# Second half of an RWKV-7 layer's projections in another order: gates first, rates among the keys

## The chip, the cores and the metric

The kernel runs on one core of one Trainium2 chip. The metric is the device time of one execution in microseconds. A core has five engines that run side by side, each with its own queue of instructions in a fixed order: PE multiplies matrices (PEld loads its stationary operands), DVE, ACT and POOL work elementwise, and SP here issues the transfers between memory and the chip. An instruction waits on semaphores for what it needs, and all instructions behind it in the same queue wait with it.

## The reference, cut to what matters

The program computes two layers over 1024 tokens of width 1024 in float32: an RWKV-7 time mixing layer and a diagonal state-space layer, each followed by a squared-ReLU MLP and a layer norm. The change is in the projections of the first one:

```python
xx = jnp.pad(x, ((0, 0), (1, 0), (0, 0)))[:, :-1] - x
xr = x + xx * mu[0]                      # and xw, xk, xv, xa, xg with mu[1..5]
r = xr @ wr
w_pre = (w0 + jnp.tanh(xw @ w1) @ w2)
decay = jnp.exp(-jnp.exp(-jax.nn.softplus(-w_pre) - 0.5))
k = xk @ wk
v = xv @ wv
a = jax.nn.sigmoid(a0 + (xa @ a1) @ a2)
g = jax.nn.sigmoid(xg @ g1) @ g2
```

Then a recurrence over the tokens uses `r`, `decay`, `k`, `v` and `a` per head, its output is normalised, multiplied by `g` and by `wo`. In the kernel the "rates" are the two small products with `w2` and `a2` (64 rows each) and the sigmoids after them, the "gates" are `g`, the "keys" are `k`, and R is `r`.

## The kernel before, in words

All activations lie transposed, features on the partitions. The 1024 tokens are worked in two halves of 512 (`H` is 0 or 1), and the 1024 features in eight tiles of 128 (`KT`). Every dense product is made in float32 precision from three products of split operands: `split` (L145 to L147) makes a high part with a copy on ACT (L146) and a low part with a subtraction on DVE (L147), and `mm3` (L177) issues high by high, high by low and low by high. All of them are recorded on L175. `wload` (L158) brings weights in pieces of 256 KB into `wraw` (two buffers) and splits them into `whi` and `wlo` (three buffers each).

`rwkv_proj(H)` (L229) makes the projections of one half. It splits the input `xs` into eight pairs of operands (`xo`), and from these makes the inner products of the rates and gates (`shifted`, L310, and `scaled`, L295): the source of the rates is `hd`, split into `hx` (L335); those of the gates are `gx` and `h2` (L355 and L336). Then come the outer products. `rates(n)` (L369) makes six matmuls on halves of the array, into two PSUM banks, and for each bank a tanh on ACT (L380), a half-sigmoid on POOL (L325) and a store (L365). `gate(n)` (L384) makes four matmuls, one copy on ACT (L397) and a store. `square(wn, out, xm, n)` (L400) makes the 24 matmuls of one tile of keys or R from the operands `xm`, a copy (L404) and a store. `mixes(j)` (L263) makes these operands: a product on ACT (L266), a multiply-add on DVE (L268) or two steps on POOL (L271, L272), and a split. The results go to memory (`s_sg`, `s_a`, `s_g`, `s_k`, `s_r`, `s_v`) and are loaded again by the units that use them.

Buffers are rings that hand out a slot when its last reader has finished. PSUM has three banks `d` for the dense products (`psd`, L214). Results on their way out, and the POOL part of `mixes`, share three buffers `ev`. For the second half the operand pairs `xo`, `hx`, `gx`, `h2` and later `xm` share one ring of eight high and eight low tiles (`oAh`, `oAl`, `optile`, L204). For the first half `hx` and the others stand in spare buffers of the recurrence (`spare`, L251).

The recurrence is worked in eight units (`core`, L757), four for each half of the tokens. A unit loads its rates, keys and R and prepares them (`elem`, L474), makes its score matrices (`amat`, L551), inverts triangular blocks, mostly on DVE (`invert`, L585), and steps through a chain of small matmuls (`chain`, L645). A unit of the second half needs the second half's projections. The kernel is ordered when it is built: a planner simulates a timeline, and gives each engine the instruction that is ready by that simulation and has the lowest number. Numbers grow in program order, and `rank` (L86) sets where they start. The units have numbers up to about 80000; the projections of the second half start at 100000 and stand in the program before unit 3 (L771 to L773), so they are filler beside the chains of units 2 and 3. The MLP of the first half of the tokens starts at 200000 and fills in later; the first half's `wo` has 99000.

Of the kernel before, what the change touches and what calls it, by code (L numbers as in the profile page):

```python
# [19 lines left out]
KT = 8  # L20
# [50 lines left out]
def trunk(ctx, tc, A):  # L71
# [13 lines left out]
    @contextmanager  # L85
    def rank(base):  # L86

        keep = tc.cur_priority
        tc.cur_priority = base
        yield  # L90
        tc.cur_priority = keep
# [53 lines left out]
    def split(src, hi, lo, e=None):  # L145
        S.copy(hi, src)  # L146
        (e or V).tensor_sub(lo, src, hi.bitcast(F32))  # L147
# [10 lines left out]
    def wload(src, kt, n):  # L158
        step = 512 // n
        out = []  # L160
        for k0 in range(0, kt, step):
            raw = wp.tile([128, step, n], F32, tag="wraw", name="wraw", bufs=2)
            SP.dma_start(raw, src[:, k0 : k0 + step])
            hi = wp.tile([128, step, n], F32R, tag="whi", name="whi")
            lo = wp.tile([128, step, n], F32R, tag="wlo", name="wlo")
            nw[0] += 1
            split(raw, hi, lo, G if nw[0] % WLG[0] in WLG[1] and WLG[2] <= nw[0] < WLG[3] else V)
            out += [(hi[:, k], lo[:, k]) for k in range(step)]
        return out
# [4 lines left out]
    def mmb(p, w, x, **kw):  # L174
        bulk.append((PE.matmul(p, w, x, **kw).ins, x.shape[-1]))  # L175
# [23 lines left out]
    def dense(p, w, xs):  # L199
        n = len(xs)  # L200
        for k in range(n):
            mm3(p, w[k][0], w[k][1], xs[k][0], xs[k][1], k == 0, k == n - 1)

    def optile(H, hl):  # L204
        if H == 1:
            return sp.tile([128, HT], F32R, tag="oB" + hl, name="oB" + hl, bufs=8)
        return ap.tile([128, HT], F32R, tag="oA" + hl, name="oA" + hl, bufs=8)
# [6 lines left out]
    def psd():  # L214
        return pd.tile([128, HT], F32, tag="d", name="d")
# [13 lines left out]
    def rwkv_proj(H):  # L229
# [21 lines left out]
        def spare(tag, n, bufs, pool=kp):  # L251
            t = pool.tile([128, n, HT], F32R, tag=tag, name="oS", bufs=bufs)
            return [t[:, k] for k in range(n)]

        def spare0():
            t = spare("vsa", 2, 2) + spare("vsa", 2, 2)
            for _ in range(4):
                t += spare("kbt", 1, KTB)
            t += [stash[:, k, l] for k in (1, 2, 3) for l in range(2)]
            t += spare("o", 1, OB) + spare("o", 1, OB)  # L260
            return [(t[2 * k], t[2 * k + 1]) for k in range(KT)]

        def mixes(j, dst=None):  # L263
            for k in range(KT):
                m = tp.tile([128, HT], F32, tag="m", name="m")
                S.mul(m, xs[k][:, 1:], mum[:, j, k : k + 1])  # L266
                if k % 4 in VM[H]:
                    V.scalar_tensor_tensor(m, xs[k][:, 0:HT], vec(f"mu{j}", k), m, op0=ALU.mult, op1=ALU.add)  # L268
                else:
                    m2 = tp.tile([128, HT], F32, tag="ev", name="m2", bufs=3)  # L270
                    G.tensor_scalar(m2, xs[k][:, 0:HT], vec(f"mu{j}", k), None, op0=ALU.mult)  # L271
                    G.tensor_add(m, m, m2)  # L272
                if dst:
                    split(m, *dst[k])
                    yield dst[k]
                else:
                    yield operand(m)
# [46 lines left out]
        def half_sigmoid(t):  # L324
            G.tensor_scalar(t, t, 0.5, 0.5, op0=ALU.mult, op1=ALU.add)  # L325
# [3 lines left out]
        if H == 0:  # L329
            stash = ap.tile([128, 2 * KB2, 2, HT], F32R, tag="q", name="stash", bufs=1)  # L330
            hx = stash[:, 0, 0], stash[:, 0, 1]
            gx, h2 = spare("gt", 1, GTB) + spare("lg", 1, LGB), spare("la", 1, 2, tp)[0]
        else:
            hx, gx, h2 = [(optile(0, "h"), optile(0, "l")) for _ in range(2)] + [optile(0, "h")]
        split(hd, *hx)  # L335
        def gate_c():  # L336

# [26 lines left out]
        def store_out(out, n, e):  # L364
            (ST if out in STO else SP).dma_start(scr[out][n * 128 : (n + 1) * 128, t0 : t0 + HT], e)  # L365
# [3 lines left out]
        def rates(n):  # L369

            if n % 4 == 0:
                w2[0] = wload(A["wa2"][:, n // 4], 4, 128)
            pp = [psd(), psd()]
            for wi, xi in ((0, 0), (0, 1), (1, 0)):
                for j in range(2):
                    js = slice(64 * j, 64 * j + 64)
                    mmb(pp[j], w2[0][n % 4][wi][js], hx[xi][js], start=wi == 0 and xi == 0, stop=wi == 1)
            for j, out in ((0, "sg"), (1, "a")):
                e = tp.tile([128, HT], F32, tag="ev", name="ev", bufs=3)
                S.activation(e, pp[j], AF.Tanh, bias=pvh[:, j, n : n + 1], scale=0.5)  # L380
                half_sigmoid(e)
                store_out(out, n, e)

        def gate(n):  # L384
            if n % 4 == 0:
                wg[0] = wload(A["g2a"][:, n // 4], 4, 128)
                rawb = wp.tile([128, 512], F32, tag="wraw", name="w2raw", bufs=2)
                SP.dma_start(rawb, A["g2b"][:, n * 128 : n * 128 + 512])
                wg[1] = wp.tile([128, 512], F32R, tag="whi", name="w2st")
                S.copy(wg[1], rawb)  # L390
                V.tensor_sub(wg[1][64:128], rawb[64:128], wg[1][64:128].bitcast(F32))
            q = n % 4
            p = psd()
            mm3(p, wg[0][q][0], wg[0][q][1], gx[0], gx[1], True, False)
            mmb(p, wg[1][:, q * 128 : (q + 1) * 128], h2, start=False, stop=True)
            e = tp.tile([128, HT], F32, tag="ev", name="ev", bufs=3)
            S.copy(e, p)  # L397
            store_out("g", n, e)

        def square(wn, out, xm, n):  # L400
            p = psd()
            dense(p, wload(A[wn][n], KT, 128), xm)
            e = tp.tile([128, HT], F32, tag="ev", name="ev", bufs=3)
            S.copy(e, p)  # L404
            store_out(out, n, e)

        if H == 0:

            km = xm
            with rank(MIX0R):  # L410
                rm = list(mixes(0, spare0()))
            for n in range(4):
                rates(n)
                square("wk", "k", km, n)
            for n in range(4):
                square("wr", "r", rm, n)
            yield
            for n in range(4, KT):
                rates(n)
                square("wk", "k", km, n)  # L420
            for n in range(4, KT):
                square("wr", "r", rm, n)
            if not GV:
                for n in range(KT):
                    gate(n)
        else:
            for n in range(KT):
                rates(n)
            for n in range(KT):
                gate(n)  # L430
            xm = list(mixes(2))
            for n in range(KT):
                square("wk", "k", xm, n)
            xm = list(mixes(0))
            for n in range(KT):
                square("wr", "r", xm, n)
# [320 lines left out]
    def core():  # L757

        pg = rwkv_proj(0)
        next(pg)  # L760
        bulk.clear()
# [8 lines left out]
        for m in range(8):  # L770
            if m == PB:  # L771
                with rank(100000):
                    run(rwkv_proj(1))  # L773
# [591 lines left out]
```

## Time and profile before

| | |
|---|---|
| median of 3 runs | 2767.67 us (2766.5 to 2772.65) |
| profiled execution | 2764.91 us |
| its span, first to last instruction | 2763.2 us |
| mean granted clock of PE | 0.958 |
| PE busy | 2604.9 us, 94% |
| DVE busy | 1884.5 us, 68% |
| ACT busy | 1109.5 us, 40% |
| POOL busy | 719.6 us, 26% |
| stores of the second half's rates | 349 to 392 us |
| of its gates, keys, R | 391 to 411, 455 to 497, 522 to 584 us |

A profile is one execution taken by the hardware profiler. Times are in microseconds from the span's start. In a row of the timeline stand start, duration, engine, line, operation, the tile written and those read, the shape and how many; in square brackets the idle time of the engine before it and what ended it. In a group's row stand busy time, the mean of one in nanoseconds, and the idle time before them with what ended it. The duration of a matmul is longer than the distance from one to the next, since they overlap.

### The profile page before, as it was taken

What the parts mean: (1) busy time and instruction counts of PE and PEld (TensorE: products, weight loads), DVE (VectorE), ACT (ScalarE), POOL (GpSimd) and SP (SyncE); (2) the same over time, 40 slices, a digit from 0 to 9 for tenths busy, and PEclk for the clock granted to TensorE, in tenths of its full rate; (3) what the DMA queues carried; (4) which work ended last, traced back from release to release, by engine and by line L of the source; (5) the groups of instructions that cost most, each with busy time, mean ns of one, the idle gap of its engine ahead of it and who ended that gap; (6) DMA issues with size and microseconds to landing.
All of it is one profiled execution on the core that took longest, in us unless ns stands there. A gap on an engine that the chain in (4) does not pass through costs nothing.

```text
span 2763.2 us, 43707 instructions
## 1 busy us (share of the span) xinstructions
PE 2604.9 (94%) x16582; PEld 2096.5 (76%) x16582; DVE 1884.5 (68%) x3242; ACT 1109.5 (40%) x1952; POOL 719.6 (26%) x601
## 2 busy tenths in 40 slices
PE   7889989889899999989999999999999999999997
PEld 5779767678677877767776788778778887788886
DVE  7487788587787777998658554574765546755556
ACT  5445454544443333334432332344323323533333
POOL 5331664450352303233122001121220101210101
PEclk9989969889889999999999999999999999999998
DMA  3543443344222323555332633223343322333333
GB/s 115 184 147 112 139 162 102 109 138 135 77 81 81 100 85 124 154 145 159 96 122 99 203 96 98 89 88 102 117 160 112 99 96 84 119 96 97 98 95 100
DMA packets 200083, 318.63 MB, mean 115 GB/s; under 512 B 19520, under 2 KB 73920, under 8 KB 199872
## 3 DMA queue, kind: packets, MB, share of 16 engines
q1 hardware_dynamic: 199872, 315.83, 36.6%
q8 instruction: 131, 2.15, 0.3%
q14 instruction: 80, 0.66, 0.1%
HBM read 265.42 MB, written 50.33 MB: 114 GB/s over the span
## 4 chain that ended last, share of the span: by engine, by line
PE 45%; DVE 5%; issue 2%; POOL 1%; DMA 1%; ACT 0%; ACTq 0%; DVEq 0%; POOLq 0%
PE d L175 40%; PE py L1219 1%; PE py L1224 1%; DVE wlo L147 1%; PE pu L152 1%; DVE t L1187 1%; PE pbu L1175 1%; DVE hA L960 0%; DVE hB L960 0%; DVE t L1185 0%; POOL rl L944 0%; PE pq L849 0%; DMA wraw<-in_mw_dram 0%; PE pu L1164 0%; DVE qbuf L147 0%
## 5 line engine op out<-in xcount | busy, mean ns | idle before, releaser
L147 DVE TENSOR_TENSOR wlo<-wraw,whi 128x512 fp32r<-128x512 f32 x720 | 535.6, 745 | 443.7 <-ACT whi L146 424.8
L146 ACT CAST whi<-wraw 128x512 fp32r<-128x512 f32 x720 | 445.7, 620 | 975.4 <-PE d L175 637.2
L175 PE MATMUL d<-qbuf,whi 128*128 128x512 f32 (+1 forms) x2112 | 655.6, 393 | 20.9 <-DVE hA L960 9.4
L175 PEld LDWEIGHTS d<-qbuf,whi 128*128 128x128 f32 x2112 | 390.3, 190 | 117.7 <-DVE hA L960 17.0
L944 POOL TENSOR_TENSOR rl<-rl 128x512 f32<-128x512 f32 x128 | 158.6, 1239 | 1058.4 <-ACT rl L943 1018.1
L175 PE MATMUL d<-qbuf,wlo 128*128 128x512 f32 (+1 forms) x1056 | 409.3, 390 | 8.2 <-DVE wlo L147 8.0
L175 PE MATMUL d<-oAh,whi 128*128 128x512 f32 (+1 forms) x960 | 387.8, 408 | 9.6 <-ACT ev L404 7.2
L175 PE MATMUL d<-oAh,wlo 128*128 128x512 f32 (+1 forms) x960 | 387.2, 406 | 5.3 <-DVE wlo L147 5.1
L175 PE MATMUL d<-oAl,whi 128*128 128x512 f32 (+1 forms) x960 | 385.5, 404 | 1.4 <-DVE oAl L147 1.4
L175 PE MATMUL d<-oBh,wlo 128*128 128x512 f32 x704 | 278.3, 396 | 1.4 <-DVE wlo L147 1.4
L175 PE MATMUL d<-oBh,whi 128*128 128x512 f32 x704 | 278.8, 396 | 0.0
L175 PE MATMUL d<-oBl,whi 128*128 128x512 f32 x704 | 276.1, 392 | 0.0
L175 PEld LDWEIGHTS d<-qbuf,wlo 128*128 128x128 f32 x1056 | 200.6, 190 | 52.8 <-DVE wlo L147 11.7
L175 PEld LDWEIGHTS d<-oAh,whi 128*128 128x128 f32 (+1 forms) x960 | 185.1, 194 | 54.2 <-ACT ev L404 9.2
L175 PEld LDWEIGHTS d<-oAh,wlo 128*128 128x128 f32 (+1 forms) x960 | 184.9, 193 | 49.1 <-DVE wlo L147 8.6
L175 PEld LDWEIGHTS d<-oAl,whi 128*128 128x128 f32 (+1 forms) x960 | 184.8, 193 | 40.6 <-DVE oAl L147 2.1
L960 DVE TENSOR_TENSOR hB<-hB,d 128x512 f32<-128x512 f32 (+1 forms) x256 | 165.2, 650 | 68.9 <-PE d L175 65.8
L960 DVE TENSOR_TENSOR hA<-hA,d 128x512 f32<-128x512 f32 x240 | 162.5, 683 | 54.5 <-PE d L175 52.5
L175 PEld LDWEIGHTS d<-oBh,wlo 128*128 128x128 f32 x704 | 132.5, 188 | 33.8 <-DVE wlo L147 2.0
L175 PEld LDWEIGHTS d<-oBl,whi 128*128 128x128 f32 x704 | 132.7, 188 | 29.4 <-issue 0.5
L175 PEld LDWEIGHTS d<-oBh,whi 128*128 128x128 f32 x704 | 132.7, 189 | 29.1 <-issue 1.5
L147 DVE TENSOR_TENSOR qbuf<-rl,qbuf 128x512 fp32r<-128x512 f32 x128 | 99.0, 774 | 70.3 <-ACT qbuf L146 69.8
(371 smaller groups left out, 3877.1 us busy)
## 6 DMA issues: line engine op xcount, KB each, us to landing
wraw<-in_mw_dram SPq DMA_DIRECT2D x520, 256.0 KB, 2.7
wraw<-in_glu_dram SPq DMA_DIRECT2D x64, 256.0 KB, 2.6
wraw<-in_wk_dram SPq DMA_DIRECT2D x32, 256.0 KB, 3.1
wraw<-in_wr_dram SPq DMA_DIRECT2D x32, 256.0 KB, 3.1
wraw<-in_wv_dram SPq DMA_DIRECT2D x32, 256.0 KB, 3.4
yl<-s_y SPq DMA_DIRECT2D x32, 256.0 KB, 3.1
wraw<-in_wo_dram SPq DMA_DIRECT2D x32, 256.0 KB, 2.8
tb<-tB SPq DMA_DIRECT2D x16, 512.0 KB, 4.9
```

The source lines that it names most:

```text
L146: S.copy(hi, src)
L147: (e or V).tensor_sub(lo, src, hi.bitcast(F32))
L152: PE.matmul(out, x, idt, start=True, stop=True)
L175: bulk.append((PE.matmul(p, w, x, **kw).ins, x.shape[-1]))
L944: G.tensor_mul(r, r, r)
L960: V.tensor_add(z, z, p)
L1175: PE.matmul(p[qs, g2, ri], tb[:, g2, ri, qs], u[:, 2 * g2 + par], start=True, stop=True)
L1187: e.tensor_mul(t2[:, :, ri], x[:, :, 1 - ri], bw[:, l, g0:g1, ri : ri + 1].broadcast_to([128, g1 - g0, n]))
L1219: PE.matmul(p[64 * j : 64 * j + 64, g2], ug[f][:, 2 * g2 + par], tv[:, par, g2], start=g2 == 0, stop=False, skip_group_check=True)
L1224: PE.matmul(p[64 * j : 64 * j + 64, g2], hb[qs, 4 * f + g2, ri, 0:NSC], tcm[qs, g2, ri], start=False, stop=ri == 1, skip_group_check=True)
```

## The change

In the second half the order of the outer products is gates, then key operands, then one tile of rates and one of keys in turn; R and V follow as before. Before it was all rates, all gates, key operands, all keys. The rates' operand pair `hx` no longer comes from the ring of eight: it gets two tiles of its own, 2 KB per partition each, in a ring `hx` of two in the pool of the recurrence. `gx` and `h2` stay in the ring of eight. The first half is unchanged; it already takes a tile of rates and one of keys in turn.

```diff
@@ -331,7 +331,7 @@
             hx = stash[:, 0, 0], stash[:, 0, 1]
             gx, h2 = spare("gt", 1, GTB) + spare("lg", 1, LGB), spare("la", 1, 2, tp)[0]
         else:
-            hx, gx, h2 = [(optile(0, "h"), optile(0, "l")) for _ in range(2)] + [optile(0, "h")]
+            hx, gx, h2 = spare("hx", 1, 2) + spare("hx", 1, 2), (optile(0, "h"), optile(0, "l")), optile(0, "h")
         split(hd, *hx)
         def gate_c():
 
@@ -425,11 +425,10 @@
                     gate(n)
         else:
             for n in range(KT):
-                rates(n)
-            for n in range(KT):
                 gate(n)
             xm = list(mixes(2))
             for n in range(KT):
+                rates(n)
                 square("wk", "k", xm, n)
             xm = list(mixes(0))
             for n in range(KT):
```

## The prediction

> **What bounds the kernel now.** I read the page first, then the busy time by stretch of the second half's projections, then the instructions of that stage in order of time.
>
> ```profile
> span 2763.2 us, 43707 instructions
> ...
> PE 2604.9 (94%) x16582; PEld 2096.5 (76%) x16582; DVE 1884.5 (68%) x3242; ACT 1109.5 (40%) x1952; POOL 719.6 (26%) x601
> ...
> PE d L175 40%; PE py L1219 1%; PE py L1224 1%; DVE wlo L147 1%; PE pu L152 1%; DVE t L1187 1%; PE pbu L1175 1%; DVE hA L960 0%; DVE hB L960 0%; DVE t L1185 0%; POOL rl L944 0%; PE pq L849 0%; DMA wraw<-in_mw_dram 0%; PE pu L1164 0%; DVE qbuf L147 0%
> ```
>
> PE is busy 94% of the span and the dense matmuls (L175) are the largest part of the chain. So an edit that moves no work off PE can win only by closing gaps of PE or by letting it run at a higher granted clock. The second view shows where such gaps are; columns are busy us of PE, PEld, DVE, ACT, POOL, then granted clock, DMA share and GB/s.
>
> ```profile
> core 0: us, PE busy (x) PEld busy (x) DVE busy (x) ACT busy (x) POOL busy (x), PEclk, DMA share, GB/s
> 300.00:345.00 45.00, 40.87 (x394) 32.60 (x393) 36.91 (x55) 18.99 (x39) 30.40 (x27) 0.89 0.40 120
> 345.00:383.60 38.60, 28.65 (x231) 20.78 (x229) 35.18 (x85) 18.63 (x35) 21.18 (x24) 0.67 0.34 116
> 383.60:410.00 26.40, 25.45 (x337) 20.99 (x336) 23.68 (x33) 16.00 (x31) 20.79 (x19) 0.76 0.75 244
> 410.00:455.00 45.00, 41.06 (x346) 32.19 (x346) 37.90 (x63) 22.76 (x44) 22.73 (x17) 0.82 0.12 38
> 455.00:500.00 45.00, 39.07 (x348) 31.76 (x344) 33.00 (x77) 21.43 (x42) 16.95 (x13) 0.94 0.59 182
> ...
> 660.00:1150.00 490.00, 462.39 (x3566) 368.59 (x3566) 395.09 (x788) 194.50 (x358) 147.15 (x119) 0.95 0.32 100
> ```
>
> From 345 to 455 PE idles 9.95 + 0.95 + 3.94 = 14.8 us of 110 and the clock is at 0.67 to 0.82; from 660 to 1150 it idles 27.6 us of 490 at 0.95. The stage of the change is thus the thin one. DVE is nearly full there: 3.4, 2.7 and 7.1 us idle in the same three stretches. The next rows, from the timeline, are the borders of the stage: first matmul of the rates (64 rows), first and last of the gates, first of the key tiles, then the first POOL step of the key operands, and the store of the last key tile.
>
> ```profile
> 345.16 0.50 PE L175 MATMUL d<-oAh,whi 64*128 64x512 f32 x1
> 383.61 0.79 PE L175 MATMUL d<-oAh,whi 128*128 128x512 f32 x1
> 409.88 0.63 PE L175 MATMUL d<-oAh,w2st 128*128 128x512 f32 x1
> 424.75 1.22 PE L175 MATMUL d<-oAh,whi 128*128 128x512 f32 x2
> ```
>
> ```profile
> 407.45 3.13 POOL L271 TENSOR_SCALAR m<-xs,pv 128x512 f32<-128x512 f32 x2 [2.04 <-DMA s_g<-ev]
> ...
> 496.58 0.33 SPq L365 DMA_DIRECT2D s_k<-ev  x1
> ```
>
> The rates hold the stage from 345 to 384, the gates to 410. The key operands (L266 to L277) start only at 407, when a gate's store gives back an `ev` buffer, so between 410 and 424.75 there is no dense matmul at all, and the first key tiles follow their operands one by one.
>
> **The change part by part.** It adds and removes no arithmetic: 48 rate, 32 gate and 192 key matmuls, 16 tanh, 16 half-sigmoids, 32 stores of rates, gates and keys and the weight loads all stay. Only their numbers in the planner's order change, and two buffers of 2 KB per partition are added. Each effect is costed on the profiled execution, 2764.91 us (span 2763.2 plus 1.7 around it), which lies 2.8 us under the median of the runs, 2767.67.
>
> *Gates first, key operands sooner: a gain.* If the gates take their present 26.4 us from 345 on, the `ev` buffers pass to the key operands at about 371 instead of 407. The first row gives the times of their last DVE step, the two below what they need of DVE, all of 415 to 500:
>
> ```profile
> L147 DVE TENSOR_TENSOR oAl<-m,oAh x8: 678/684/1767, 421.0 to 449.4; 128x512 fp32r<-128x512 f32 x8
> ...
> L147 DVE TENSOR_TENSOR oAl<-m,oAh 128x512 fp32r<-128x512 f32 x8 | 6.4, 821 | 0.1
> L268 DVE SCALAR_TENSOR_TENSOR m<-xs,pv,m 128x512 f32<-128x512 f32 x4 | 3.6, 890 | 0.0
> ```
>
> Together 10.0 us. DVE's idle time from 371.4 to 410 is 12.2/38.6 of 3.4, or 1.1, plus 2.7: 3.8 us, because the inversion and the chains, with lower numbers, go first. So 3.8 of 10.0 us can be done ahead of 410. If DVE alone sets the pace, the keys move forward by 3.8 us; if the operands' elapsed time counts (407.45 to the last operand's DVE step at 449.4, 42 us), by 38% of it, 16 us. DVE is 84% busy from 410 to 455, nearer the first end: I take 8.
>
> *Rates' operands in their own tiles: a small gain.* Before, they share the ring of the layer-input operands and wait until a slot of it is free:
>
> ```profile
> 302.12 0.63 ACT L328 ACTIVATE hd<-hd 64x512 f32<-64x512 f32 x1 [1.05 <-DVE hd L321]
> ...
> 321.33 0.62 ACT L146 CAST oAh<-hd 128x512 fp32r<-128x512 f32 x1
> ```
>
> The source is ready at 302.7 and copied at 321.3, 18.6 us later. With own tiles a few rates can run before 345, where PE idles 4.1 us; that is the upper end, zero the lower. POOL, which each rate tile needs twice, is busy 30.4 of 45 us there: I take 2.
>
> *Rates among the key tiles: a loss.* A rate tile takes two of the three PSUM banks `d`, so the key tile after it must wait for the copy of the one before. The first half of the sequence already runs in this order, and its right-hand tiles (R) run without rates:
>
> ```profile
> 62.37 0.33 SPq L365 DMA_DIRECT2D s_k<-ev  x1
> ...
> 90.83 0.32 SPq L365 DMA_DIRECT2D s_k<-ev  x1
> ...
> 96.36 0.32 SPq L365 DMA_DIRECT2D s_r<-ev  x1
> ...
> 113.11 0.33 SPq L365 DMA_DIRECT2D s_r<-ev  x1
> ```
>
> Three steps of keys take 28.5 us, three of R 16.8: 9.5 against 5.6 us a tile. The waits of that stage (60 to 92), and of the next four tiles (115 to 155), where elementwise and score work stands beside them, name the bank:
>
> ```profile
> PE d L175 <- ACT ev L404: 5.7, 3, 4.0
> ```
>
> ```profile
> PE d L175 <- ACT ev L404: 1.5, 2, 0.9
> ```
>
> Over four tiles that is 1.4 or 0.4 us a tile, for eight tiles 11 or 3 us. The second half has a chain and an inversion beside it as the second row has: I take 3. What hides the rest is this small PE work; without it 11 are due. The rate weights now also occupy one of the three `whi`/`wlo` pairs through all key tiles, which is in those same tiles' steps. The 16 stores of the rates move too, on SP's queue: at 0.33 us (the row of a key's store) 5.3 us of issuing go in among the key weights' loads. I cost that at nothing, as SP has only issues to do; but a store that waits for its half-sigmoid holds back the weight loads behind it, which belongs to the first rival.
>
> *Half-sigmoids beside the weight splits: a small loss.* 16 of them move from beside the inversion (345 to 384) to beside the key weights' DVE step. This step has a longer mean where POOL is busy (345 to 415, first two rows) than at 415 to 500 (third):
>
> ```profile
> L325 POOL TENSOR_SCALAR ev<-ev 128x512 f32<-128x512 f32 x16 | 11.7, 742 | 14.4 <-issue 7.8 <-ACT ev L380 6.5
> L147 DVE TENSOR_TENSOR wlo<-wraw,whi 128x512 fp32r<-128x512 f32 x4 | 4.4, 1101 | 1.1 <-ACT whi L146 1.1
> ...
> L147 DVE TENSOR_TENSOR wlo<-wraw,whi 128x512 fp32r<-128x512 f32 x16 | 11.0, 693 | 7.7 <-ACT whi L146 7.7
> ```
>
> 16 splits at 0.408 us more are 6.5 us of DVE; zero is the other end, since the inversion is freed of the same. DVE idles 12 us from 455 to 500, which hides most: I take 1. The Trainium skill, SBUF — State Buffer, section "SBUF: two separate sides", gives the reason: VectorE with two SBUF inputs and a reading GpSimd operation exclude each other for a whole instruction. By it at most all 11.7 us of POOL would land on DVE; the difference of the two rows agrees with it in kind.
>
> *Sum:* −8 − 2 + 3 + 1 = −6 us, 2758.9 in a profiled execution, 2761.7 as a median. I carry it to the end in full, because PE's later work keeps its order and the MLP's matmuls wait as filler. The second half's wo starts at 1144 behind twelve of the MLP's blocks while the last chain step is well before it:
>
> ```profile
> L674 ACT COPY o<-pR x28: 353/373/375, 312.8 to 1057.5; 128x256 f32<-128x256 f32 x28
> ```
>
> ```profile
> L928 DVE SCALAR_TENSOR_TENSOR hB<-hB,d x8: 674/680/682, 1144.4 to 1204.1; 128x512 f32<-128x512 f32 x8
> ```
>
> So the chains have some 80 us from their last step to that point for what remains of them, and need not move for the gain to last. Between 2 and 12 us of gain is the forecast's own range: 2756 to 2766.
>
> **The rivals.** *Slower: POOL's queue holds the rates.* The next unit's key factor (L529) waits in POOL's order for the key tiles to come back from memory:
>
> ```profile
> 463.28 1.36 POOL L529 TENSOR_TENSOR kf<-kf,ldk 128x512 f32<-128x512 f32 x1 [16.02 <-DMA ldk<-s_k]
> ```
>
> Before, every half-sigmoid is past by then. After, those of rates 2 to 7 belong to the same time. If the planner puts one behind such a wait, its `ev` buffer and with three of them the banks stay taken, and the key tiles stop: 16.0 us for one such wait, less the gain of 6, is +10: 2778 as a median; with a second wait of this kind (the unit loads its keys twice) +26. It decides as soon as one half-sigmoid stands behind L529. Against it: the planner has the low numbers go first only when it believes them ready.
>
> *No change.* DVE, 129.8 of 155 us busy from 345 to 500, sets this stage, so what is gained early is waited for later; or the planner, which takes what is ready, still runs the rates ahead of the gates (ready at 303 against 345), and the order hardly differs. 0 ± 4: 2768.
>
> *Larger gain: the clock.* If key matmuls fill 400 to 425, the lost clock of 383.6 to 455 comes back too: 26.4 × 0.24 + 45 × 0.18 = 14.4 us, together −20: 2747. For it: PE was 25.45 of 26.4 us busy at 0.76, so the clock itself was the limit there. Against it: DVE. The Trainium skill, TensorE: Matmul & The Clock Gate, section "HAM oscillation — how this bites in real kernels", says that idle stretches above about 3.4 us bring the low clock; by it the idle of 345 to 384, left by the chain's hops and not by the order of the filler, keeps the clock low, which speaks against this rival.
>
> **How the numbers follow.** Forecast 0.38, larger gain 0.11, no change 0.23, slower 0.28. A measurement here tells 0.2%, 5.5 us, from no change. The forecast's range lies on both sides of 2762.2; I give 0.27 of it to faster and 0.11 to same; the larger gain adds 0.11 to faster; no change splits into 0.05 faster, 0.13 same and 0.05 slower: faster 0.43, same 0.24, slower 0.28 + 0.05 = 0.33. The likeliest gives 2762. The range reaches down past the larger gain, to 2744, and up to 2786, beyond one POOL wait and the 11 us of banks less the gains.
>
> **What would show it.** Right: gates' matmuls first at about 345, L271 of the second half at about 371, first key matmul before 415, last key store before 490, PE idle and DVE idle of 345 to 410 smaller. Wrong: L325 with a long idle time behind L529; L147 of the weights above 0.8 us on average through the key tiles; waits of L175 for L404; a last key store later than 497; or a gain at 500 that is gone at 1144, which would mean that the chains set the time there.

## The result, and the profile after

The changed kernel is slower: 2783.47 us as a median of 8 runs (2774.82 to 2792.15), the kernel before 2767.76 us (8 runs, 2756.45 to 2774.54). The ratio is 1.0053, with a 95% interval of 1.0039 to 1.0067, or some 15 us. The forecast was 2762 us; the time lies in the range and on the wrong side of no change. The profiled execution took 2783.82 us.

The page of the changed kernel has nearly the same busy time as before on every engine (PE 2602.1 against 2604.9 us) and a longer span:

```profile
span 2782.0 us, 43698 instructions
...
PE 2602.1 (94%) x16582; PEld 2092.8 (75%) x16582; DVE 1883.5 (68%) x3242; ACT 1107.9 (40%) x1952; POOL 714.3 (26%) x601
```

So no work was added: PE's idle time grew from 158.3 to 179.9 us, and its mean granted clock is 0.957 after 0.958. The busy time by stretch says where. First the changed kernel, with the columns that the prediction names:

```profile
0.00:300.00 300.00, 259.71 (x1919) 210.40 (x1919) 199.78 (x386) 151.20 (x272) 106.51 (x110) 0.95 0.45 140
...
300.00:345.00 45.00, 39.61 (x330) 30.14 (x328) 36.97 (x52) 18.29 (x37) 30.27 (x25) 0.89 0.42 127
345.00:383.60 38.60, 31.28 (x325) 23.51 (x324) 34.18 (x64) 23.45 (x46) 25.49 (x19) 0.89 0.38 119
383.60:410.00 26.40, 21.18 (x81) 14.18 (x82) 26.22 (x44) 11.65 (x19) 20.23 (x17) 0.51 0.31 96
410.00:455.00 45.00, 42.92 (x454) 33.37 (x454) 34.46 (x85) 24.22 (x45) 11.49 (x15) 1.00 0.45 144
455.00:500.00 45.00, 38.69 (x462) 30.13 (x459) 31.80 (x70) 22.93 (x46) 22.43 (x20) 0.89 0.38 124
500.00:590.00 90.00, 80.16 (x674) 63.05 (x673) 61.74 (x97) 36.67 (x70) 37.91 (x31) 0.89 0.34 109
590.00:660.00 70.00, 50.69 (x459) 46.90 (x457) 58.94 (x105) 28.70 (x49) 31.38 (x27) 0.71 0.41 121
660.00:1150.00 490.00, 460.39 (x3647) 372.46 (x3646) 380.72 (x784) 195.09 (x361) 149.24 (x120) 0.94 0.34 103
1150.00:1300.00 150.00, 135.02 (x757) 103.63 (x756) 139.16 (x201) 66.64 (x103) 53.62 (x39) 0.99 0.58 160
```

And the rows of the kernel before that the prediction did not show:

```profile
0.00:300.00 300.00, 265.79 (x1941) 214.65 (x1942) 203.37 (x393) 153.30 (x276) 109.26 (x112) 0.95 0.44 142
...
500.00:590.00 90.00, 79.70 (x659) 64.24 (x660) 58.57 (x87) 41.16 (x78) 47.35 (x36) 0.88 0.36 115
590.00:660.00 70.00, 65.64 (x634) 61.68 (x633) 55.09 (x115) 32.18 (x58) 19.38 (x18) 0.88 0.43 133
...
1150.00:1300.00 150.00, 133.39 (x724) 101.43 (x723) 137.71 (x202) 67.74 (x104) 61.20 (x43) 0.93 0.56 146
```

Busy time times granted clock is a measure of how much PE got done. Made from these rows (the clock has two digits, so the rows of 300 and 490 us are good to some 2 us each):

| stretch | before | after | difference |
|---|---|---|---|
| 0 to 300 | 252.5 | 246.7 | −5.8 |
| 300 to 500 (five rows) | 145.3 | 151.2 | +5.9 |
| 500 to 590 | 70.1 | 71.3 | +1.2 |
| 590 to 660 | 57.8 | 36.0 | −21.8 |
| 660 to 1150 | 439.3 | 432.8 | −6.5 |
| 1150 to 1300 | 124.1 | 133.7 | +9.6 |

Together −17.4 of the 18.8 us. The first row isn't the change's: three later kernels with the same edit (changed_v_first, changed_rn_behind_v, changed_v_on_dve) have 263 to 265 us of PE in that stretch; this execution was late from the start. Where the change acts, 300 to 500, PE does 5.9 us more, but this is no sign of the forecast gain by itself: it makes up for the late start, and the three later kernels, which did not start late, do some 2 us more there (147.5 to 147.7 against 145.3). The largest deficit is one stage further on: from 590 to 660, where V's products are due, PE idles 19.3 of 70 us where it idled 4.4, at a clock of 0.71 where it had 0.88.

The projections did move as meant. The rows are the first gate matmul, POOL's first step of the key operands (four of them, with the first and last start), and the last store of a key tile:

```profile
344.98 0.48 PE L175 MATMUL d<-oAh,whi 128*128 128x512 f32 x1
...
L271 POOL TENSOR_SCALAR m<-xs,pv x4: 1559/1686/2035, 365.4 to 373.4; 128x512 f32<-128x512 f32 x4
...
491.10 0.32 SPq L365 DMA_DIRECT2D s_k<-ev  x1
```

The key operands begin at 365 instead of 407 and the keys end at 491 instead of 497. What paid for it is unit 2's inversion, which lies in the same stretch. It is a chain of 30 pairs of short DVE steps (L608 and L610 before, L607 and L609 after) between two transposes. Before:

```profile
352.28 1.97 DVE L600 STREAM_TRANSPOSE xa<-x 128x1024 f32<-128x1024 f32 x1 [1.24 <-ACT x L599]
...
389.26 1.25 DVE L615 STREAM_TRANSPOSE XT<-x 128x1024 f32<-128x1024 f32 x1
...
L610 DVE TENSOR_TENSOR x<-x x30: 174/260/1285, 357.1 to 384.1; 128x110 f32<-128x110 f32 x3, 128x120 f32<-128x120 f32 x3, 128x30 f32<-128x30 f32 x2, 128x56 f32<-128x56 f32 x2
...
400.74 0.37 ACT L674 COPY o<-pR 128x256 f32<-128x256 f32 x1
```

After, with a piece of DVE's order from within the chain:

```profile
359.19 2.06 DVE L599 STREAM_TRANSPOSE xa<-x 128x1024 f32<-128x1024 f32 x1
...
374.75 0.26 DVE L607 TENSOR_TENSOR x<-xa,x 128x110 f32<-128x110 f32 x1
374.93 0.68 DVE L147 TENSOR_TENSOR oAl<-m,oAh 128x512 fp32r<-128x512 f32 x1
375.53 0.67 DVE L712 TENSOR_REDUCE sm<-o 128x8 f32<-128x512 f32 x1
376.13 0.94 DVE L609 TENSOR_TENSOR x<-x 128x110 f32<-128x110 f32 x1
...
423.79 1.25 DVE L614 STREAM_TRANSPOSE XT<-x 128x1024 f32<-128x1024 f32 x1
...
L609 DVE TENSOR_TENSOR x<-x x30: 174/272/1225, 364.4 to 422.4; 128x110 f32<-128x110 f32 x3, 128x120 f32<-128x120 f32 x3, 128x30 f32<-128x30 f32 x2, 128x56 f32<-128x56 f32 x2
...
434.69 0.37 ACT L673 COPY o<-pR 128x256 f32<-128x256 f32 x1
```

The median step is hardly longer, 272 against 260 ns, but the 30 of them take 58 us where they took 27: between the two steps of a pair now stand a low part of a key operand and a step of a normalisation (L712, in `gnorm`). From transpose to transpose the inversion takes 64.6 us instead of 37.0, and the first copy of unit 2's chain (L674 before, L673 after) comes 34 us later (400.7 to 434.7). The key operands are not all that stands in the gaps. DVE's rows between the two transposes add up to this, before and after: the inversion's own steps 24.2 and 27.6 us, key operands 0 and 11.2, the preparation of the next unit 5.4 and 12.9, low parts of weights 1.0 and 4.8, normalisation 3.5 and 6.9, the multiplications of the scores by their mask 0 and 2.0.

The third reading is POOL's queue at V's operands (L271 and L272). Before, a first pair of V's products stands ahead of unit 5's power step (L510):

```profile
578.14 3.54 POOL L271 TENSOR_SCALAR m<-xs,pv 128x512 f32<-128x512 f32 x2
...
586.27 1.67 POOL L510 TENSOR_TENSOR rn<-rn,mhalf 128x8 f32<-128x8 f32 x1 [3.36 <-DVE rn L509]
```

After, the power step (now L509) stands ahead of them, and POOL sits idle for 15.4 us until DVE has its input:

```profile
584.57 1.65 POOL L509 TENSOR_TENSOR rn<-rn,mhalf 128x8 f32<-128x8 f32 x1 [15.36 <-DVE rn L508]
586.21 3.11 POOL L271 TENSOR_SCALAR m<-xs,pv 128x512 f32<-128x512 f32 x2
...
643.26 1.08 SPq L457 DMA_DIRECT2D s_v<-evv  x2
...
L927 DVE SCALAR_TENSOR_TENSOR hA<-hA,d x8: 675/686/689, 710.0 to 767.3; 128x512 f32<-128x512 f32 x8
L927 DVE SCALAR_TENSOR_TENSOR hB<-hB,d x8: 679/680/683, 1185.5 to 1246.0; 128x512 f32<-128x512 f32 x8
```

The first store of V is at 643 (before 619), the first half's `wo` at 710 (before 682), the second half's at 1185 (before 1144). PE's waits from 575 to 650 name the operands (total us, times, longest); before, they were 1.3 and 3.2 us:

```profile
PE d L175 <- ACT oAh L146: 8.2, 1, 8.2
...
PE d L175 <- DVE oAl L147: 6.7, 2, 4.2
```

### The profile page after: what moved, and what is told of

Its sections match the earlier page's. It is cut to its first block, busy times and chain, and to the rows that moved or that the text cites. A ratio compares the mean times of both kernels' runs of the same rounds, so it can differ in the third digit from the quotient of the medians.

```text
span 2782.0 us, 43698 instructions
## 1 busy us (share of the span) xinstructions
PE 2602.1 (94%) x16582; PEld 2092.8 (75%) x16582; DVE 1883.5 (68%) x3242; ACT 1107.9 (40%) x1952; POOL 714.3 (26%) x601
## 4 chain that ended last, share of the span: by engine, by line
PE 60%; DVE 16%; issue 5%; DMA 4%; ACT 2%; POOL 1%; SPq 0%; ACTq 0%; DVEq 0%; POOLq 0%
PE d L175 51%; DVE wlo L147 3%; DMA wraw<-in_mw_dram 2%; PE py L1218 1%; DVE x L607 1%; DVE x L609 1%; PE py L1223 1%; PE pA L566 1%; DVE hA L959 1%; PE pu L152 1%; POOL rl L943 1%; PE pbu L1174 1%; ACT whi L146 1%; DMA ldsg<-s_sg 1%; DVE oAl L147 1%
## 5 line engine op out<-in xcount | busy, mean ns | idle before, releaser
L147 DVE TENSOR_TENSOR wlo<-wraw,whi 128x512 fp32r<-128x512 f32 x720 | 541.4, 753 | 452.1 <-ACT whi L146 432.2
L175 PE MATMUL d<-oAh,whi 128*128 128x512 f32 x944 | 384.7, 409 | 16.5 <-ACT ev L404 9.7
L175 PE MATMUL d<-oAl,whi 128*128 128x512 f32 x944 | 384.1, 407 | 9.9 <-DVE oAl L147 9.9
L175 PE MATMUL d<-oAh,wlo 128*128 128x512 f32 x944 | 382.1, 405 | 4.7 <-DVE wlo L147 4.6
L175 PEld LDWEIGHTS d<-oAh,whi 128*128 128x128 f32 x944 | 182.7, 194 | 62.2 <-ACT ev L404 11.9
L175 PEld LDWEIGHTS d<-oAl,whi 128*128 128x128 f32 x944 | 183.5, 194 | 52.3 <-DVE oAl L147 14.2
L175 PEld LDWEIGHTS d<-oAh,wlo 128*128 128x128 f32 x944 | 183.8, 195 | 46.8 <-DVE wlo L147 7.2
```

## The experiments

The theory after this reading: the key operands, ready during unit 2's inversion, are put by the planner between its steps; the chains start late, POOL's order at V changes, V's operands come late and PE has nothing to do. The rivals: the `hx` tiles, the turns of rates and keys (PSUM banks, half-sigmoids), or the lateness of V as a matter of its number alone. Each kernel below is compared with runs of the kernel before on the same chip; its 95% interval stands in brackets.

**The tiles alone.** The kernel before with only the first hunk of the change.

```diff
-            hx, gx, h2 = [(optile(0, "h"), optile(0, "l")) for _ in range(2)] + [optile(0, "h")]
+            hx, gx, h2 = spare("hx", 1, 2) + spare("hx", 1, 2), (optile(0, "h"), optile(0, "l")), optile(0, "h")
```

> The kernel before with the rates' operands in two tiles of their own, and nothing else: rates, gates, key operands, keys as before. Theory A (the loss of 15.7 us comes from the key operands being made while DVE steps through the inversion of unit 2; they start at 365 instead of 407, that inversion takes 65 us instead of 37, and chains 2 and 3 run 34 and 22 us later): the order is as before, so the inversion of unit 2 takes 35 to 45 us and the time is within 6 us of before. Theory B (the tiles themselves, by a shifted plan of everything after, cost it): 8 to 16 us slower than before.

Measured: 1.0014 [1.0002, 1.0025]. The inversion takes 36.7 us as before (transposes at 352.05 and 388.78). The source of the rates is copied at 302.13, right behind its tanh, yet the first rate is stored at 349.1 as before (349.3). The tiles bring no gain, if anything they cost 4 us, and they aren't the loss of 15.

**Gates first, without the turns.** The changed kernel with all rates ahead of the key operands.

```diff
-            xm = list(mixes(2))
             for n in range(KT):
                 rates(n)
+            xm = list(mixes(2))
+            for n in range(KT):
                 square("wk", "k", xm, n)
```

> The changed kernel without the turn-taking: gates, all rates, key operands, all keys. Gates are still first and the operands of the rates in their own tiles. Theory A: the key operands stand behind the rates again and start only at about 395 to 410, after the inversion of unit 2, so it takes 35 to 45 us and the time is within 6 us of before. Theory C (gates ahead of rates cost it, since unit 4 gets its rates later): 8 to 16 us slower than before.

Measured: 1.0002 [0.9991, 1.0013]. The low parts of the key operands fall to 408 to 429, behind the inversion, and none of their DVE steps stands in it. Even so it takes 48.4 us (353.87 to 402.32), with more of the other work between its steps than before (preparation of a unit 9.6 us, normalisation 6.4, low parts of weights 3.8); chain 2 starts at 411.6, 11 us later than before, and V's stage is nearly full:

```profile
590.00:660.00 70.00, 63.20 (x628) 59.17 (x627) 53.27 (x111) 32.26 (x56) 16.69 (x16) 0.90 0.42 129
```

So neither the gates' place nor the tiles make the loss. A chain that is 11 us late costs nothing that can be measured here, unless gates first gain what it costs; the run doesn't tell these apart.

**Early key operands, without the turns.** The changed kernel with the key operands where the change has them, and all rates ahead of all keys.

```diff
             for n in range(KT):
                 rates(n)
+            for n in range(KT):
                 square("wk", "k", xm, n)
```

> The changed kernel with the key operands as early as in it, straight behind the gates, but all rates ahead of all keys. Theory A: the inversion of unit 2 is stretched to 55 us or more, chain 2 starts after 425, and the time is 8 to 20 us above before, like the change. Theory D (the turns of rates and keys on three banks cost it): without turns it is within 6 us of before, whatever the inversion takes.

Measured: 1.0095 [1.0077, 1.0113]. The inversion is as long as in the changed kernel (359.14 to 424.56, 65.4 us), chain 2 starts at 433.7, and V's first store is at 653. It differs from the run before it in one line, which makes the key operands ahead of the rates: that takes the inversion from 48.4 to 65.4 us and the time from no loss to a loss. The turns of rates and keys are not needed for it; with them the loss is smaller (1.0053 against 1.0095). What else makes this order worse than the change's wasn't followed up: here the keys wait for all rates, and the first R store is at 534 instead of 523, so part of this loss may be R's.

**The inversion slowed, nothing else.** The kernel before, with an in-place copy on ACT (0.2 us) of one strip of the triangular block after each of the 30 steps of unit 2's inversion. The values stay the same, DVE gets no work, and rates, gates and keys keep their order.

```diff
             V.tensor_add(xv[:, s + 1 : 32, 0:w], xv[:, s + 1 : 32, 0:w], tv)
+            if D.m == 2:
+                S.copy(xv[:, s + 1 : s + 2, 0:w], xv[:, s + 1 : s + 2, 0:w])
```

> The kernel before with one copy of a small strip in place on ACT after each of the 30 steps of unit 2's inversion: it adds hops to ACT and no work on DVE; rates, gates and keys keep their order. Theory A (the stretch of this inversion by itself sets off the loss): the inversion takes 55 to 75 us instead of 37, chain 2 starts 20 us or more later, and the time is 8 to 20 us above before though the key operands are made as before. Rival F (the stretch is harmless, and early key operands cost through something else): within 5 us of before.

Measured: 1.0056 [1.0044, 1.0068], the same loss as the change's. Its inversion takes 58.4 us (354.41 to 412.85), chain 2 starts at 426.3, and the later marks are those of the changed kernel, a little weaker: POOL idle ahead of the power step, thin PE at 590 to 660, `wo` late (from 699.7). The keys are not late (last store 485, before 497), nor is R (582, before 584).

```profile
L610 DVE TENSOR_TENSOR x<-x x30: 204/275/1331, 359.2 to 408.9; 128x110 f32<-128x110 f32 x3, 128x120 f32<-128x120 f32 x3, 128x30 f32<-128x30 f32 x2, 128x56 f32<-128x56 f32 x2
...
576.43 1.65 POOL L510 TENSOR_TENSOR rn<-rn,mhalf 128x8 f32<-128x8 f32 x1 [13.02 <-DVE rn L509]
...
590.00:660.00 70.00, 55.41 (x530) 51.64 (x531) 58.84 (x119) 29.27 (x50) 24.88 (x22) 0.80 0.39 123
```

This is the run that carries the theory: a longer inversion of unit 2 is enough for a loss of this size, with the rates, gates and keys in their old order and no key operand within it.

**The key operands kept out of the inversion.** Two ways. In the first, the DVE steps of the key operands stand in DVE's order behind the inversion's last transpose (shown for the multiply-adds; the low parts are treated alike, and the helper `after_inv` that sets the order is left out):

```diff
-                    V.scalar_tensor_tensor(m, xs[k][:, 0:HT], vec(f"mu{j}", k), m, op0=ALU.mult, op1=ALU.add)
+                    i = V.scalar_tensor_tensor(m, xs[k][:, 0:HT], vec(f"mu{j}", k), m, op0=ALU.mult, op1=ALU.add)
+                    if inv is not None:
+                        after_inv(i, inv)
```

> The changed kernel with one more order on DVE alone: the multiply-add and the subtraction of the second half's key operands stand behind the last transpose of unit 2's inversion in DVE's queue. Theory A: that inversion takes 35 to 45 us again, chain 2 starts near 400, and the time is 8 us or more below the change, at or under before. Rival E (the loss arises from 590 on, where V's operands are made during the inversion of unit 4, and has nothing to do with unit 2): inversion 2 is short again, but the time stays within 6 us of the change.

Measured: 1.0100 [1.0079, 1.0121]. In the second, DVE makes none of their steps, POOL makes the multiply-adds and the low parts:

```diff
-                if k % 4 in VM[H]:
+                if k % 4 in VM[H] and not pool:
...
-                    yield operand(m)
+                    yield operand(m, 0, G if pool else None)
```

> The changed kernel with the second half's key operands made on ACT and POOL alone: the four multiply-adds and eight subtractions of DVE (10 us) go to POOL. Theory A: the inversion of unit 2 is shortened from 65 to under 52 us, chain 2 starts before 422, and the time is 5 us or more below the change. Rival (POOL is then the next to be late, or POOL's reads hold DVE up as much as its own work did): the inversion stays above 55 us and the time is at the change or above.

Measured: 1.0163 [1.0149, 1.0176]. Both shorten the inversion (to 50 and 47 us) and both are slower than the change, so neither undoes the loss. They brought losses of their own: in the first the operands, waiting half made, hold the `ev` buffers that the rates need (POOL's products of 371.65 and 375.00 are added only at 413 and 420), and the rates are stored from 420 to 508; in the second POOL is the late engine, with rates from 427 to 522 and R up to 617. They settle nothing about the inversion. That undoing its stretch regains the time is therefore shown only by the order gates, rates, keys, which makes the key operands later altogether.

**V earlier by its number.** Changed and before, with V's operands at a number below the units' (32000), so that the planner prefers them.

```diff
-        xv = list(mixes(3))
+        if H == 0:
+            xv = list(mixes(3))
+        else:
+            with rank(32000):
+                xv = list(mixes(3))
```

> The changed kernel with V's operands of the second half given a low number (32000, ahead of the preparation, the scores and the inversion of unit 4) and nothing else. Theory A2 (the last link of the loss is that V's operands are made late, at 605 to 637 instead of 589 to 616, because the delayed chain 3 and its normalisation and the inversion of unit 4 go first on DVE and POOL, so that PE idles 19 of 70 us from 590 to 660): V's operands are done by about 620, PE idle from 590 to 660 falls below 10 us and the time falls by 8 us or more against the change. Rival (it is R's and the keys' progress that sets the time, V only shows it): within 5 us of the change.

> The kernel before with the same low number for V's operands. Theory A2: V's operands are not late there, so it gains less than 5 us or nothing, and the difference between this and the changed kernel with the same edit is under 8 us. Rival: it gains as much as the changed kernel does, so that the 15.7 us between them stay.

Measured: changed 1.0057 [1.0045, 1.0068], before 0.9998 [0.9983, 1.0014]. No effect: in the changed one POOL still idles 12.4 us ahead of the power step (at 578.54), and PE has 53.91 of 70 us. So V is not late for want of a better number; presumably the planner's timeline had the power step ready at once, but that was not looked at.

**The power step behind V's second product.** Changed, and the kernel with the slowed inversion, each with unit 5's power step ordered behind V's second product on POOL (`vfirst[0]`; the lines that note it in `mixes` are left out).

```diff
-            G.tensor_tensor(rn, rn, mhalf[:, 0:8], op=ALU.pow)
+            i = G.tensor_tensor(rn, rn, mhalf[:, 0:8], op=ALU.pow)
+            if D.m == 5 and j == 0:
+                tc.add_manual_dep(i.ins, vfirst[0], mybir.DependencyInfo(
+                    mybir.DependencyClass.NoSync, mybir.DependencyReason.DATA), reason="v")
```

> The changed kernel with one order on POOL alone: the power step of unit 5's first key norm (rn, L509 there), which waits 15.4 us for DVE with V's first products behind it in POOL's queue, stands behind the second of these products. Theory G (the last link of the loss is this place in POOL's queue): V's first products start at about 570 instead of 586, V's first operands are split before 598 instead of 605, PE idle from 590 to 660 falls from 19 to under 13 us, and the time is 5 us or more below the change (1.0053 becomes under 1.0035). Rival (DVE, which steps through the inversion of unit 4 from 580 on, holds V's operands whatever POOL does): 0 to 3 us below the change.

> The kernel before with the slowed inversion of unit 2 (1.0056 by itself) and the same order on POOL. Theory G: also here 5 us or more of the 15.5 us come back. Rival: 0 to 3 us.

Measured: 1.0027 [1.0012, 1.0042] and 1.0033 [1.0018, 1.0048]; both regain some 0.25%, about half of the loss (0.26 and 0.23%, each with an uncertainty of some 0.2% from the two intervals together). But POOL's rows of the first show that one wait gave way to two others:

```profile
576.60 2.05 POOL L271 TENSOR_SCALAR m<-xs,pv 128x512 f32<-128x512 f32 x1 [10.54 <-DMA s_r<-ev]
...
589.28 1.57 POOL L271 TENSOR_SCALAR m<-xs,pv 128x512 f32<-128x512 f32 x1 [5.33 <-ACT kbt L586]
```

The first product runs at 564.46 now, but the second waits for an `ev` buffer that an R store holds, V's last DVE step is at 626 all the same, and from 590 to 660 PE has 53.33 us, as little as with changed_v_first. So this order matters to the time, but the gain doesn't come through the stretch where I looked for it. The traces place it only in time: in both kernels the first half's `wo` ends no sooner with this order, but the second half's starts sooner (at 1170, against 1180 in changed_v_first, and at 1169 against 1175 in the slowed pair).

**V without POOL.** Changed and before, with all multiply-adds of the second half's V operands on DVE.

```diff
-                if k % 4 in VM[H]:
+                if k % 4 in VM[H] or (H == 1 and j == 3):
```

> The changed kernel with V's operands of the second half made without POOL (all eight multiply-adds on DVE, 2.8 us more of DVE, 11 us less of POOL). Theory G: no queue of POOL stands before them, they start some 8 to 12 us sooner, and the time is 5 us or more below the change. Rival (DVE and its inversion hold them): no gain, or up to 5 us slower.

> The kernel before with V's operands of the second half made by DVE alone, no POOL step (the computed values stay the same). changed_v_on_dve, the changed kernel with the same edit, kept 1.0037 although its V stores (607 to 667 us) and its PE busy time of 590 to 660 (63.76 us) are those of the kernel before. Theory A, the late V operands were the whole loss and V on DVE has a price of its own: V on DVE takes DVE time from the units' work (four multiply-adds at 0.89 us and what they push behind them), so the kernel before with it is slower by about as much, 1.002 to 1.004. Theory B, a part of the loss lies elsewhere in the change: in the kernel before POOL does not hold V up (its L271 stands ahead of the rn step), so V's operands move by less than 10 us and the ratio is 0.998 to 1.001; then 7 to 10 us of the change's loss are not V's. If it is below 0.998 the edit is worth having by itself.

Measured: changed 1.0037 [1.0025, 1.0049], before 1.0019 [1.0004, 1.0033]. In the changed kernel V's operands are done by 602 us (638 without the edit), the thin stretch is repaired almost altogether, and `wo` starts a little earlier than before (682.3):

```profile
590.00:660.00 70.00, 63.76 (x596) 59.57 (x595) 51.63 (x108) 25.94 (x47) 19.81 (x19) 0.88 0.50 158
...
L927 DVE SCALAR_TENSOR_TENSOR hA<-hA,d x8: 679/685/687, 679.2 to 735.3; 128x512 f32<-128x512 f32 x8
```

That V's operands starve PE from 590 to 660 is thus shown. That this stretch is where the time is lost is not: with it repaired the time falls by only 0.16% (1.0053 to 1.0037), with an uncertainty of 0.18%. The edit has a price of its own, though, 0.19% in the kernel before, where V was not late. Less that price the changed kernel is 0.18% slower, with an uncertainty of 0.19% (the two intervals together): the rest of the loss can't be told from nothing, if the two effects add, which no run shows.

The kernel before with this edit shows one thing more. It has V and the first half's `wo` 14 us earlier than before, and is slower in the end:

```profile
660.00:1300.00 640.00, 585.85 (x4162) 462.94 (x4161) 523.09 (x963) 250.88 (x445) 209.64 (x161) 0.93 0.36 109
...
L928 DVE SCALAR_TENSOR_TENSOR hA<-hA,d x8: 676/683/689, 668.0 to 723.4; 128x512 f32<-128x512 f32 x8
L928 DVE SCALAR_TENSOR_TENSOR hB<-hB,d x8: 673/680/681, 1148.2 to 1208.6; 128x512 f32<-128x512 f32 x8
```

In the kernel before that stretch is this:

```profile
660.00:1300.00 640.00, 595.78 (x4288) 470.02 (x4288) 532.80 (x989) 262.24 (x461) 208.35 (x161) 0.95 0.38 111
```

The lead of 14 us at 668 is gone at 1148, where the second half's `wo` starts 4 us later than before (1144): PE idles 54.2 us from 660 to 1300 instead of 44.2, at 0.93 instead of 0.95. My reading is that filler done early is missing later. No version beat the kernel before; gates_rates_keys equals it, and so does before_v_first.

## Why the prediction was wrong, point by point

**The step that failed** is in the first term of the sum: "DVE's idle time from 371.4 to 410 is 12.2/38.6 of 3.4, or 1.1, plus 2.7: 3.8 us, because the inversion and the chains, with lower numbers, go first. So 3.8 of 10.0 us can be done ahead of 410." The groups of the changed kernel from 345 to 410 show all of it done by then (columns: busy us, mean ns, then idle time before):

```profile
L147 DVE TENSOR_TENSOR oAl<-m,oAh 128x512 fp32r<-128x512 f32 x8 | 6.3, 793 | 0.0
L268 DVE SCALAR_TENSOR_TENSOR m<-xs,pv,m 128x512 f32<-128x512 f32 x4 | 4.9, 1230 | 0.0
```

That is 11.2 us, and all of it stands between the inversion's steps. A lower number wins only among instructions that are ready, and a chain of dependent steps has at any time just one that is ready or none. So whatever else is ready can go between two steps; that the planner's timeline decided so was not looked at, but the result is in the rows: the two steps that read 128x110 start 0.3 us apart before (363.51 and 363.81) and 1.4 us apart after (374.75 and 376.13), with two instructions of 0.7 us between. The inversion grew by 27.6 us. Of these, some 11 come without any key operand in it (gates_rates_keys), from the preparation of the next unit, the normalisation and the weights; the rest comes when the key operands are made early (keys_ready_early). I had priced what DVE would give to the keys and nothing for what the chain would lose to them.

**The gain of the keys, −8.** Right for the keys, not for PE: the keys end 6 us earlier in this execution, which began late, and 10 to 11 in the three later kernels with the same edit, but PE does only some 2 us more from 300 to 500 in those.

**Own tiles, −2.** Wrong by itself: +0.14% [+0.02, +0.25], some 4 us slower. The 18.6 us of waiting for a slot are gone, but no rate came sooner.

**Banks, +3.** Too large. PE's waits for the copy of a key tile, which was the term, come to 0.6 us from 410 to 500:

```profile
PE d L175 <- ACT ev L404: 0.6, 2, 0.3
```

With 0.3 us for a rate's tanh (L380) that is 0.9 us from 340 to 500, and 0 before.

**Half-sigmoids beside the weight splits, +1.** About right, at most. From 402 to 500, with 14 of the 16 half-sigmoids there, a split takes 722 ns, and 692 in the row of 410 to 500 before:

```profile
L147 DVE TENSOR_TENSOR wlo<-wraw,whi 128x512 fp32r<-128x512 f32 x17 | 12.3, 722 | 9.8 <-ACT whi L146 7.4 <-PE d L175 2.4
...
L147 DVE TENSOR_TENSOR wlo<-wraw,whi 128x512 fp32r<-128x512 f32 x17 | 11.7, 692 | 7.7 <-ACT whi L146 7.7
```

17 times 0.030 is 0.5 us. The rule of the Trainium skill that the prediction weighed (SBUF — State Buffer, "SBUF: two separate sides") allows up to a whole POOL instruction for each split; here the two hardly met: two of the 17 splits ran beside a half-sigmoid, and took 1.09 and 0.68 us. Where it may show is in the multiply-adds of the key operands, which took 1230 ns on average ahead of 410, with POOL busy 45.7 of 65 us, and 890 before.

**"I carry it to the end in full."** Wrong in both directions. The keys' gain was gone at the last R store (590 against 584, and 582 to 586 in the three later kernels with the same edit), and a lead of 14 us at `wo` in before_v_on_dve came to nothing. The argument was that the chains have some 80 us to spare before the second half's `wo` "and need not move for the gain to last". They did have time: their last step is at 1048 us after, 1057 before, although chain 2 began 34 us late. So the time was not lost at the end of the chains but on the way, by what PE lacked while they were late; V at 590 to 660 is the one place found. The start of the second half's `wo`, 41 us later, is not a measure of it: in own_tiles_only it is 22 us late (1166) in a kernel that is some 4 us slower.

**The rivals.** The slower one named the right kind, an instruction that waits in POOL's queue with needed work behind it, and nearly the length of the wait (16 us; measured 15.4). The length is chance: the rival's wait was for keys from memory, with half-sigmoids behind the key factor, and the measured one is for DVE, with V's products behind the power step. The half-sigmoids waited 17.2 us in all from 410 to 500, but for their own tanh on ACT, in the row "ev L325" of that stretch:

```profile
POOL ev L325 <- ACT ev L380: 17.2, 4, 9.3
```

That POOL starts its instructions in order is what the Trainium skill states too (PSUM — Partial Sum Buffer, "Engine vs sequencer instructions"); the trace agrees, in that the L271 at 586.21 follows the power step at 584.57, while with the order turned round it ran at 564.46. The larger gain by the clock came true for one stretch (410 to 455: 1.00 instead of 0.82) and was taken back by two others (383.6 to 410: 0.51 for 0.76; 590 to 660: 0.71 for 0.88). The argument against it, that the idle time of 345 to 384 would stay and keep the clock low, did not hold: PE idles 7.3 us there instead of 9.95, at 0.89 instead of 0.67. The case of no change didn't happen, and the gates did go first.

**What is shown and what is not.** Shown by runs: a longer inversion of unit 2 alone makes a loss of this size (1.0056 against 1.0053); making the key operands early lengthens it by 17 us and brings a loss (gates_rates_keys against keys_ready_early); late V operands make the thin stretch; neither the tiles nor the gates' place makes the loss, and the turns are not needed for it. Not shown: that taking the key operands out of the changed kernel's inversion, and nothing else, regains the time (two attempts had losses of their own). Open: by which road the late chains cost the time. V is the one seen in the traces, but the stretch repaired regains 0.16% with an uncertainty of 0.18%, and the power step's order regains 0.25% while the stretch stays.

## What to carry to other kernels

Work made ready earlier is not free where it shares an engine with a serial chain of short dependent steps: price it by what it does to that chain, step by step, and then follow the chain's end to the next place where a queue's order depends on it. The engine's free time was no bound for that here (3.8 us free, 11.2 us put in): a long instruction between two short steps is paid by the chain. And a gain in the middle of a kernel counts only if the filler isn't missed later: look for the next thin stretch before carrying it to the end.

## What the runs showed that was not expected

An inversion some 11 us longer (48.4 against 37.0, gates_rates_keys) came with no loss that could be measured, and one some 21 us longer (58.4, before_slow_inversion) with 0.56%. The order of POOL's queue at V differs between the two: V's first product stands ahead of the power step in the one (its L271 is at 574.75) and behind it in the other. That would make the loss a step rather than a slope. It is not shown: the two kernels differ in more than the inversion, no run lies between them, and putting the order right by hand regained only about half.
